# Sample attention of a two-layer decoder step: queries as the 32-column left operand in four column groups, cached keys and values streamed

## The chip, the cores and the metric

The kernel runs on one NeuronCore of a Trainium2 chip. The metric is the device time of one execution in microseconds (us). Three runs of the kernel before gave 3340.89, 3345.87 and 3353.46 us; the median is 3345.87 us.

## The reference, cut to what matters

One inference step goes through two layers for 1024 prompt tokens and for 8 samples of 8 new tokens. The second layer is a dilated sliding-window attention with three groups of heads. The change touches only the samples' part of it:

```python
WINDOWS = (128, 512, 2048)
DILATIONS = (1, 4, 16)
def dilated_group(q, kv, start, dil, n_keys, bias):
    q_pos = start + jnp.arange(Tq)
    idx = q_pos[:, None] - dil * jnp.arange(n_keys)[None, :]
    kvg = kv[:, jnp.maximum(idx, 0)]
    s = jnp.einsum('bqhgd,bqkhd->bqhgk', q, kvg[:, :, :, 0]) * HEAD_DIM ** -0.5
    s = jnp.where(valid[None, :, None, None, :], s + bias, -jnp.inf)
    m = jnp.max(s, axis=-1, keepdims=True)
    p = jnp.exp(s - m)
    l = jnp.sum(p, axis=-1, keepdims=True)
    o = jnp.einsum('bqhgk,bqkhd->bqhgd', (p / l), kvg[:, :, :, 1])
```

A sample's query at token t reads, in group 1 (window 512, step 4), only the cached rows of one residue class modulo 4, and in group 2 (window 2048, step 16) only one of the 8 classes that its 8 tokens need. Group 0 has one class.

## The kernel before, in words

All three groups of the samples are computed in `cross` (L1533), beside the prompt's attention. `cross` walks twelve stages: the groups in the order 2, 1, 0, and in each the four heads of keys c. In a stage `attend` (L1126) computes the prompt's attention for one head and yields at many points; at each yield `advance` (L1550) lets side generators go some steps: `proj_cq` (the next stage's query projection, whose matmuls are recorded at L166, L169 and L170), the sample generators of the group just finished, and in the last group `merge` and the output projection. So the samples of group 2 run beside the prompt's group 1 (1.9 steps to one of `attend`), those of group 1 beside the prompt's group 0 (1.35 steps), and those of group 0 at the end. Within this, a scheduler fixes the order of every engine when the program is built; each engine then runs its list in that order. Weight tiles of the projections, prompt scores (L1172 for group 2, L1174 and L1175 for the others), transposes (L1204, L1116, L1415) and prompt values (L1213) are all in TensorE's one list.

`sample` (L1364) is one sample b of one group g. Its queries are the 128 columns of `qb`, in the order pair p (2), token t (8), then 8 heads. It goes through these steps:

- `fetch(0)` loads the cached keys, L1416 transposes them on TensorE into `kts`, so that they stand as d rows by 128 keys for each class r and pair p.
- L1428: for each class r and pair p, the 128x128 keys are the left operand (the weights) and the few query columns of that class are streamed: 8 columns for group 2, 16 for group 1, 64 for group 0. The helper `cols` picks them. The result `pst` is keys by queries.
- L1430 copies `pst` to SBUF on ScalarE, L1433 transposes it, L1434 adds the scores of the 8 new tokens, L1436 and L1437 add the bias, find the maximum and take the exponential.
- L1440 and L1441 transpose the probabilities; L1442 and L1443 copy them into `pT` and `pTn`.
- L1449 and L1453, both recorded at the helper's L154 (`mmc`, which keeps the matmuls of a chain in order): values as left operand, the 8 or 16 columns of `pT` streamed; then the new tokens' values with 16 rows. L1454 copies the result `po` on ScalarE and L1455 stores it.

All of these are float32. Each float32 matmul that is not a transpose stands in the trace as two records, each with its own weight load; a float32r matmul stands as one. The tiles `pst`, `ps`, `pp`, `po` and the key transposes come from four PSUM banks (tag `aux`), which the prompt's scores use too.

Of the kernel before, what the change touches and what calls it, by code (L numbers as in the profile page):

```python
# [10 lines left out]
AF = mybir.ActivationFunctionType  # L11
ALU = mybir.AluOpType

P = 128
# [93 lines left out]
class Kern:  # L108
# [1255 lines left out]
    def sample(self, g, b, qd, kn, sb, tags):  # L1364

        nc = self.nc
        mm = nc.tensor.matmul
        n = CLASSES[g]
        step = WIN[g] // P

        def fetch(kv):
            cw = self.i[f"cache_win{g + 1}"][b, :, kv].rearrange("(m r) c d -> m r (c d)", r=step)
            res = []
            for x in range(0, n, 4):
                w = min(4, n - x)
                t = self.wslot(tags[x // 4])
                nc.sync.dma_start(out=t[:, :w * 256].rearrange("m (r n) -> m r n", r=w), in_=cw[:, x:x + w])
                res.append(t)
            return res

        def cls(ts, r, p):
            return ts[r // 4][:, (r % 4) * 256 + p * P:(r % 4) * 256 + (p + 1) * P]

        def cols(t, r):
            if g == 0:
                return t
            if g == 2:
                return t[:, r * 8:(r + 1) * 8]
            return t.rearrange("k (e r x) -> k r e x", e=2, r=4)[:, r]

        def half(t, p):
            return t[:, p * 64:(p + 1) * 64]

        if g:
            ks = fetch(0)
            yield
        else:
            kv = self.wslot(tags[0])
            nc.sync.dma_start(out=kv[:, :512], in_=self.i["cache_win1"][b].rearrange("m e c d -> m (e c d)"))
            ks, vs = [kv], [kv[:, 256:512]]  # L1400
            yield
        sc = self.wslot("wh") if self.free and tags[0] == "wh" else self.tl("sc", [P, 656])
        st = pT = o = sc[:, 0:128]
        s, pTn, vn = sc[:, 128:272], sc[0:16, 272:400], sc[0:16, 400:656]
        for p in range(2):
            nc.sync.dma_start(out=vn[p * NS:(p + 1) * NS], in_=self.kvn[g][b * NS:(b + 1) * NS, 256:512])
        kts = []
        for x, src in enumerate(ks):
            t = self.wslot(tags[x]) if g else kv[:, 512:768]
            w = min(1024, n * 256)  # L1410
            for x0 in range(0, w, 512):
                xw = min(512, w)
                pk = self.ps("spp")
                for y in range(0, xw, P):
                    nc.tensor.transpose(pk[:, y:y + P], src[:, x0 + y:x0 + y + P], self.ident)  # L1415
                if x0:  # L1416
                    nc.vector.tensor_copy(t[:, x0:x0 + xw], pk[:, :xw])
                else:
                    nc.scalar.activation(t[:, x0:x0 + xw], pk[:, :xw], AF.Copy)
                yield  # L1420
            kts.append(t)
        if g:
            vs = fetch(1)
        qb = qd[:, b * P:(b + 1) * P]
        pst = self.ps("sa")
        for r in range(n):
            for p in range(2):
                mm(cols(half(pst, p), r), lhsT=cls(kts, r, p), rhs=cols(half(qb, p), r), start=True, stop=True)  # L1428
            yield
        nc.scalar.activation(st, pst[:, :P], AF.Copy)  # L1430
        yield
        ps = self.ps("sa")
        nc.tensor.transpose(ps[:, :P], st, self.ident)  # L1433
        mm(ps[:, P:P + 2 * NS], lhsT=qb, rhs=kn.rearrange("d (p t) -> d p t", p=2)[:, :, b * NS:(b + 1) * NS], start=True, stop=True)  # L1434
        nm, l = self.sml[:, g, 0, b:b + 1], self.sml[:, g, 1, b:b + 1]
        nc.vector.tensor_tensor_reduce(s, ps[:, :P + 2 * NS], sb[:, ::-1], -1.0, 1e38, ALU.add, ALU.min, nm)  # L1436
        nc.scalar.activation(s, s, AF.Exp, bias=nm, scale=-1.0, accum_out=l)  # L1437
        yield
        pp = self.ps("spp")
        nc.tensor.transpose(pp[:, :P], s[:, :P], self.ident)  # L1440
        nc.tensor.transpose(pp[0:2 * NS, P:2 * P], s[:, P:], self.ident)  # L1441
        nc.scalar.activation(pT, pp[:, :P], AF.Copy)  # L1442
        nc.vector.tensor_copy(pTn, pp[0:2 * NS, P:2 * P])  # L1443
        yield
        po = self.ps("spo")
        ch = []
        for p in range(2):
            for r in range(n):
                self.mmc(ch, cols(half(po, p), r), lhsT=cls(vs, r, p), rhs=cols(half(pT, p), r), start=not ch, stop=False)  # L1449
                if r % 2:  # L1450
                    yield
        for p in range(2):
            self.mmc(ch, half(po, p), lhsT=vn[:, p * P:(p + 1) * P], rhs=half(pTn, p), start=False, stop=p == 1)  # L1453
        nc.scalar.activation(o, po[:, :P], AF.Copy)  # L1454
        nc.sync.dma_start(out=self.os[g][:, b * P:(b + 1) * P], in_=o)  # L1455
        yield
# [76 lines left out]
    def cross(self, u):  # L1533
# [38 lines left out]
        self.ready, self.halves = [0] * 4, [[] for _ in range(4)]  # L1572
        self.merged, self.part, self.sampling = 0, [[], []], 4
        marks = []
        q = []
        for _ in self.proj_cq(u, *seq[0], q):
            pass
        for x, (c, g) in enumerate(seq):
# [7 lines left out]
            else:  # L1586
                qn = []
# [30 lines left out]
    def run(self):  # L1618
        tc = self.tc
        self.setup()  # L1620
        self.side, self.ticked = [], 0
        with tc.tile_pool(name="p1", bufs=1) as self.pool:
            self.bufs = {"Y": 16, "Y2": 8, "H": 13, "T": 7}
            self.layer0()
            u = [[None] * 3 for _ in range(KD)]
            late = self.out_proj(0, u, 1, 2)
            u1 = [[None] * 3 for _ in range(KD)]
            late = self.ffn(0, u, late, lambda c, ys: self.finish_norm(c, ys, 3, u1, None))
            self.kv_group(u1, 0, [0])
            self.kv_group(u1, 1, [0])  # L1630
            self.kv_group(u1, 0, [1])
            late()
            self.kv_group(u1, 1, [1])
            self.kv_group(u1, 0, [2])
            self.kv_group(u1, 1, [2])
            self.bias_rows()
            self.kv_group(u1, 2, [0, 1, 2])
        with tc.tile_pool(name="p3", bufs=1) as self.pool:
            self.bufs = {"Q": 6, "KT": 2, "K": 1, "V": 2, "bias": 5, "S": 6, "PT": 4, "row": 2, "st": 3, "ex": 2, "rs": 1, "sel": 1, "qn": 1, "sc": 1}
            self.three = False  # L1640
            self.cross(u1)
            self.three, self.free = True, False
        with tc.tile_pool(name="p4", bufs=1) as self.pool:
            self.bufs = {"Y": 16, "Y2": 8, "H": 13, "T": 7}
            late = self.out_proj(1, u, 5, 6)
            late = self.ffn(1, u, late, self.finish_out)
            late()
        assert not self.shifts
# [65 lines left out]
```

## Time and profile before

| what | before |
|---|---|
| median of 3 runs | 3345.87 us |
| the profiled execution's own time | 3352.04 us |
| its span, first to last instruction | 3350.3 us |
| TensorE matmul busy, share of the span | 97% |
| VectorE / ScalarE busy | 49% / 36% |
| mean granted TensorE clock | 0.979 |
| sample matmuls of groups 1 and 2 (L1428, L154) | first at 1810.5 us, last before 2410 us |

TensorE's busy time is a sum of modelled pipelined records that overlap, so the time that a matmul really takes is read from the start of one to the start of the next, in the timeline. In a timeline row the columns are start, length of the merged records, engine, source line, operation, output and inputs, and the shapes: `128*8` ahead of `128x128` would be rows by columns of the weights, the second shape is the streamed operand. A granted clock of 1.00 is 2.4 GHz, 0.50 is 1.2 GHz.

### The profile page before, as it was taken

To read this page: it belongs to the slowest core of one execution; us is meant where nothing else is said; L and a number is where in the kernel's file an instruction comes from. 1 tells how busy PE (TensorE), PEld (TensorE's weight loads), DVE (VectorE), ACT (ScalarE), POOL (GpSimd) and SP (SyncE) were. 2 spreads that over 40 slices of the span, in tenths; PEclk is the share of its full clock that TensorE was granted. 3 is DMA by queue.
4 is the path that set the end of the run, shared out by engine and by line. 5 is a ranking of instruction groups with operands and counts; after the bars stand their busy time and mean duration, and the time that the engine had idled before them with its cause. 6 is when DMAs were issued, how large, how long until landed. Compare 5 with 4: busy or idle time off the path is not lost.

```text
span 3350.3 us, 51862 instructions
## 1 busy us (share of the span) xinstructions
PE 3262.6 (97%) x20130; PEld 3095.3 (92%) x20130; DVE 1643.8 (49%) x4041; ACT 1220.1 (36%) x3016; POOL 137.3 (4%) x138
## 2 busy tenths in 40 slices
PE   8999999999999999999999999999989999999999
PEld 7899999999999999977888998887788999999998
DVE  5666554533333333462446555766685333333335
ACT  4533334431111111232576665655654211111113
POOL 0000000000000000010000000011111000000000
PEclk9999999999999999999999998988999999999999
DMA  5122234422222222234323443433442322221203
GB/s 179 41 75 73 79 113 156 126 98 70 95 70 82 92 73 70 101 126 135 100 64 95 122 127 85 119 109 92 125 125 91 111 70 88 87 75 63 61 26 110
DMA packets 362410, 318.12 MB, mean 95 GB/s; under 512 B 91208, under 2 KB 346268, under 8 KB 360732
## 3 DMA queue, kind: packets, MB, share of 16 engines
q1 hardware_dynamic: 348472, 302.07, 29.3%
q10 hardware_dynamic: 13596, 12.34, 1.2%
q8 instruction: 158, 2.59, 0.3%
q14 instruction: 88, 0.72, 0.1%
q0 software_dynamic: 96, 0.39, 0.0%
HBM read 251.44 MB, written 107.33 MB: 107 GB/s over the span
## 4 chain that ended last, share of the span: by engine, by line
PE 47%; ACT 3%; DVE 3%; issue 2%; DMA 1%; POOL 1%; SPq 0%; DVEq 0%; ACTq 0%; POOLq 0%
PE mm L166 5%; PE mm L170 5%; PE mm L169 5%; PE aux L166 5%; PE aux L170 5%; PE aux L169 5%; PE mx L1213 2%; PE aux L154 2%; PE mx L170 1%; PE mx L169 1%; PE aux L1428 1%; PE mx L166 1%; PE mx L1204 1%; PE aux L1174 1%; PE nrm L1204 1%
## 5 line engine op out<-in xcount | busy, mean ns | idle before, releaser
L166 PE MATMUL aux<-u,wh 128*128 128x384 f32 (+1 forms) x2112 | 695.8, 330 | 2.5 <-ACT u L220 2.5
L169 PE MATMUL aux<-u,wh 128*128 128x384 f32 (+1 forms) x2112 | 696.1, 330 | 0.0
L170 PE MATMUL aux<-u,wl 128*128 128x384 f32 (+1 forms) x2112 | 695.4, 330 | 0.0
L166 PE MATMUL mm<-u,wh 128*128 128x384 f32 (+1 forms) x1152 | 409.0, 356 | 12.0 <-ACT u L220 10.0
L166 PEld LDWEIGHTS aux<-u,wh 128*128 128x128 f32 x2112 | 397.5, 188 | 3.5 <-ACT u L220 3.5
L169 PEld LDWEIGHTS aux<-u,wh 128*128 128x128 f32 x2112 | 397.6, 188 | 0.3 <-DVE u L221 0.3
L170 PEld LDWEIGHTS aux<-u,wl 128*128 128x128 f32 x2112 | 397.3, 188 | 0.0
L169 PE MATMUL mm<-u,wh 128*128 128x384 f32 (+1 forms) x1152 | 392.5, 341 | 3.3 <-DVE u L221 3.2
L170 PE MATMUL mm<-u,wl 128*128 128x384 f32 (+1 forms) x1152 | 392.6, 341 | 0.0
L926 DVE TENSOR_TENSOR aux<-g,aux 128x384 f32<-128x384 f32 x132 | 71.4, 541 | 610.7 <-PE aux L170 422.6
L91 ACT ACTIVATE wh<-ws 128x1024 fp32r<-128x1024 f32 (+1 forms) x177 | 184.3, 1052 | 445.3 <-PE aux L169 277.5
L92 DVE TENSOR_TENSOR wl<-ws,wh 128x1024 fp32r<-128x1024 f32 (+1 forms) x177 | 215.3, 1225 | 200.2 <-ACT wh L91 199.8
L166 PEld LDWEIGHTS mm<-u,wh 128*128 128x128 f32 x1152 | 223.4, 194 | 23.1 <-ACT u L220 11.5
L169 PEld LDWEIGHTS mm<-u,wh 128*128 128x128 f32 x1152 | 223.0, 194 | 8.7 <-DVE u L221 4.7
L166 PE MATMUL mm<-h,wh 128*128 128x384 f32 (+1 forms) x704 | 230.4, 328 | 0.0
L169 PE MATMUL mm<-h,wh 128*128 128x384 f32 (+1 forms) x704 | 230.3, 327 | 0.0
L170 PE MATMUL mm<-h,wl 128*128 128x384 f32 (+1 forms) x704 | 230.2, 327 | 0.0
L170 PEld LDWEIGHTS mm<-u,wl 128*128 128x128 f32 x1152 | 223.0, 194 | 2.6 <-issue 0.2
L925 ACT ACTIVATE g<-aux 128x384 f32<-128x384 f32 x132 | 61.9, 469 | 432.2 <-PE aux L170 432.2
L945 DVE TENSOR_TENSOR y<-y,mm 128x384 f32<-128x384 f32 (+1 forms) x320 | 168.7, 530 | 101.5 <-PE mm L170 101.3
L927 ACT ACTIVATE h<-aux 128x384 fp32r<-128x384 f32 x132 | 62.0, 469 | 385.9 <-DVE aux L926 385.9
L1179 DVE CUSTOM_DVE_ANT_0 S<-aux,bias 128x128 f32<-128x128 f32 (+1 forms) x384 | 121.6, 349 | 106.6 <-PE aux L1175 44.6
(311 smaller groups left out, 6051.2 us busy)
## 6 DMA issues: line engine op xcount, KB each, us to landing
ws<-in_w_gate_up_dram SPq DMA_DIRECT2D x88, 512.0 KB
out_dram<-in_cache_win_dram SPq DMA_DIRECT2D x64, 510.0 KB
x<-in_cache_win_dram SPq DMA_DIRECT2D x48, 512.0 KB
ws<-in_w_down_dram SPq DMA_DIRECT2D x44, 512.0 KB
ws<-in_w_in_a_dram SPq DMA_DIRECT2D x24, 512.0 KB
ws<-in_w_q_b_dram SPq DMA_DIRECT2D x24, 512.0 KB
hT<-y SPq DMA_DIRECT2D x48, 192.0 KB
og<-row SPq DMA_DIRECT2D x64, 128.0 KB
```

The lines of the kernel that those rows point to most:

```text
L91: nc.scalar.activation(v[1][:, :, :w], v[0][:, :, :w], AF.Copy)
L92: nc.vector.tensor_sub(v[2][:, :, :w], v[0][:, :, :w], v[1][:, :, :w].bitcast(F32))
L154: m = self.nc.tensor.matmul(*args, **kw)
L166: m = mm(out, lhsT=w[0], rhs=x[0], start=start, stop=False)
L169: mm(out, lhsT=w[0], rhs=x[1], start=False, stop=False)
L170: mm(out, lhsT=w[1], rhs=x[0], start=False, stop=stop)
L926: nc.vector.tensor_mul(pu[:, :n], t[:, :n], pu[:, :n])
L927: nc.scalar.activation(h[:, :n], pu[:, :n], AF.Copy)
L945: nc.vector.tensor_add(ys[m][c][:, :n], ys[m][c][:, :n], ps[:, :n])
L1179: nc.vector.tensor_tensor_reduce(s[:, :w], pv, bias[hq][:, :w][:, ::-1], -1.0, 1e38, ALU.add, ALU.min, row[:, hq:hq + 1])
L1204: m = nc.tensor.transpose(pp[:, x * P:(x + 1) * P], pr[hq][:, kt * P:(kt + 1) * P], self.ident)
L1213: m = mm(po, lhsT=v[kt].rearrange("p e d -> p (e d)"), rhs=pT[kt][x], start=x == kt == 0, stop=x == 1 and kt == nk - 1)
```

## The change

Only groups 1 and 2 change; group 0 keeps its code. Scores and values are now both computed by `classes`: the left operand is a slice of 32 columns (of the queries, or of the transposed probabilities), which goes into one of four column groups of the array and writes PSUM partitions 32x to 32x+31; the streamed operand is 128 columns of keys or of values. Four such matmuls (x = 0 to 3, one in each column group) fill one 128x128 block i of a PSUM bank, and i runs over four blocks. A block holds the products of all queries with class i, of which only the rows whose token belongs to the class are wanted. `pick` takes them: four VectorE operations in a chain, each multiplying a block by a 0/1 column of `mine` and adding the sum so far. `mine` is made once in `cross`. For the scores the sum is written into PSUM in place of the transpose of L1433. For the values, the new tokens' product `pn` is copied to SBUF, the four blocks are added to it, and one new transpose turns the result back into the layout that is stored.

```diff
--- before.py
+++ after.py
@@ -1381,13 +1381,6 @@
         def cls(ts, r, p):
             return ts[r // 4][:, (r % 4) * 256 + p * P:(r % 4) * 256 + (p + 1) * P]
 
-        def cols(t, r):
-            if g == 0:
-                return t
-            if g == 2:
-                return t[:, r * 8:(r + 1) * 8]
-            return t.rearrange("k (e r x) -> k r e x", e=2, r=4)[:, r]
-
         def half(t, p):
             return t[:, p * 64:(p + 1) * 64]
 
@@ -1423,14 +1416,43 @@
             vs = fetch(1)
         qb = qd[:, b * P:(b + 1) * P]
         pst = self.ps("sa")
-        for r in range(n):
+
+        def classes(out, left, right):
+
+
+            for i in range(4):
+                for x in range(4):
+                    p, r = x // 2, i if g == 1 else x % 2 * 4 + i
+                    xs = slice(x * 32, x * 32 + 32)
+                    mm(out[xs, i * P:(i + 1) * P], lhsT=left[:, xs], rhs=cls(right, r, p), start=True, stop=True)
+                yield
+                if g == 2:
+                    yield
+
+        def pick(out, src, other, own):
+
+            for i in range(4):
+                dst = out if i == 3 else own
+                if other is None:
+                    nc.vector.tensor_scalar(dst, src[:, :P], self.mine[:, 0:1], None, ALU.mult)
+                else:
+                    nc.vector.scalar_tensor_tensor(out=dst, in0=src[:, i * P:(i + 1) * P], scalar=self.mine[:, i:i + 1],
+                                                   in1=other, op0=ALU.mult, op1=ALU.add)
+                other = own
+
+        if g:
+            yield from classes(pst, qb, kts)
+        else:
             for p in range(2):
-                mm(cols(half(pst, p), r), lhsT=cls(kts, r, p), rhs=cols(half(qb, p), r), start=True, stop=True)
+                mm(half(pst, p), lhsT=cls(kts, 0, p), rhs=half(qb, p), start=True, stop=True)
             yield
-        nc.scalar.activation(st, pst[:, :P], AF.Copy)
+            nc.scalar.activation(st, pst[:, :P], AF.Copy)
         yield
         ps = self.ps("sa")
-        nc.tensor.transpose(ps[:, :P], st, self.ident)
+        if g:
+            pick(ps[:, :P], pst, None, s[:, :P])
+        else:
+            nc.tensor.transpose(ps[:, :P], st, self.ident)
         mm(ps[:, P:P + 2 * NS], lhsT=qb, rhs=kn.rearrange("d (p t) -> d p t", p=2)[:, :, b * NS:(b + 1) * NS], start=True, stop=True)
         nm, l = self.sml[:, g, 0, b:b + 1], self.sml[:, g, 1, b:b + 1]
         nc.vector.tensor_tensor_reduce(s, ps[:, :P + 2 * NS], sb[:, ::-1], -1.0, 1e38, ALU.add, ALU.min, nm)
@@ -1443,13 +1465,21 @@
         nc.vector.tensor_copy(pTn, pp[0:2 * NS, P:2 * P])
         yield
         po = self.ps("spo")
+        if g:
+            yield from classes(po, pT, vs)
+            pn = self.ps("sa")
+            for p in range(2):
+                mm(pn[p * 64:(p + 1) * 64, :P], lhsT=half(pTn, p), rhs=vn[:, p * P:(p + 1) * P], start=True, stop=True)
+            w = s[:, :P]
+            nc.vector.tensor_copy(w, pn[:, :P])
+            pick(w, po, w, w)
+            yield
+            po = self.ps("spp")
+            nc.tensor.transpose(po[:, :P], w, self.ident)
         ch = []
-        for p in range(2):
-            for r in range(n):
-                self.mmc(ch, cols(half(po, p), r), lhsT=cls(vs, r, p), rhs=cols(half(pT, p), r), start=not ch, stop=False)
-                if r % 2:
-                    yield
-        for p in range(2):
+        for p in range(0 if g else 2):
+            self.mmc(ch, half(po, p), lhsT=cls(vs, 0, p), rhs=half(pT, p), start=not ch, stop=False)
+        for p in range(0 if g else 2):
             self.mmc(ch, half(po, p), lhsT=vn[:, p * P:(p + 1) * P], rhs=half(pTn, p), start=False, stop=p == 1)
         nc.scalar.activation(o, po[:, :P], AF.Copy)
         nc.sync.dma_start(out=self.os[g][:, b * P:(b + 1) * P], in_=o)
@@ -1572,6 +1602,9 @@
         self.ready, self.halves = [0] * 4, [[] for _ in range(4)]
         self.merged, self.part, self.sampling = 0, [[], []], 4
         marks = []
+        self.mine = self.tl("mine", [P, 4])
+        self.nc.vector.tensor_reduce(out=self.mine, in_=self.ident.rearrange("p (a i x) -> p i a x", i=4, x=8), op=ALU.add,
+                                     axis=mybir.AxisListType.XY)
         q = []
         for _ in self.proj_cq(u, *seq[0], q):
             pass
@@ -1636,7 +1669,7 @@
             self.bias_rows()
             self.kv_group(u1, 2, [0, 1, 2])
         with tc.tile_pool(name="p3", bufs=1) as self.pool:
-            self.bufs = {"Q": 6, "KT": 2, "K": 1, "V": 2, "bias": 5, "S": 6, "PT": 4, "row": 2, "st": 3, "ex": 2, "rs": 1, "sel": 1, "qn": 1, "sc": 1}
+            self.bufs = {"Q": 6, "KT": 2, "K": 1, "V": 2, "bias": 5, "S": 6, "PT": 4, "row": 2, "st": 3, "ex": 2, "rs": 1, "sel": 1, "qn": 1, "sc": 1, "mine": 1}
             self.three = False
             self.cross(u1)
             self.three, self.free = True, False
```

The built program has 192 matmuls at L1428 and 192 at L154 of groups 1 and 2 before, in 110 uninterrupted runs of TensorE's list. Now it has 512 at L1427, in 102 uninterrupted runs: 63 of four, 17 of eight, and 22 of other lengths. Between a sample's last score matmul and the transpose of its probabilities (L1462) the list now holds some 26 to 78 other matmuls, and between the new tokens' matmuls (L1472) and the new transpose (L1478) some 15 to 33.

TensorE, the scores of the second sample of group 2 before (`mm` is a projection, `mx` the prompt's values, `aux_17632` is `pst`, the `x` tiles are keys and queries):

```order
L170 MATMUL mm_17511<-u_13472,wl_16619 128x384
L1428 MATMUL aux_17632<-x_17105,x_17571 128x8 x4
L1213 MATMUL mx_17637<-PT_17589,V_17142 128x512
L1213 MATMUL mx_17637<-PT_17590,V_17142 128x512
L1213 MATMUL mx_17637<-PT_17618,V_17142 128x512
L166 MATMUL mm_17656<-u_13430,wh_16606 128x384
L1213 MATMUL mx_17637<-PT_17619,V_17142 128x512
L169 MATMUL mm_17656<-u_13431,wh_16606 128x384
L170 MATMUL mm_17656<-u_13430,wl_16607 128x384
L1428 MATMUL aux_17632<-x_17105,x_17571 128x8 x4
```

Four matmuls stand in a run. Each loads 128x128 keys as weights and streams the eight query columns of one class through them.

TensorE, the same place now (`aux_17644` is `pst`):

```order
L1427 MATMUL aux_17644<-x_17583,x_17107 32x128
L1427 MATMUL aux_17644<-x_17608,x_17107 32x128
L1427 MATMUL aux_17644<-x_17583,x_17107 32x128
L1427 MATMUL aux_17644<-x_17608,x_17107 32x128
L1213 MATMUL mx_17649<-PT_17595,V_17144 128x512
L1213 MATMUL mx_17649<-PT_17596,V_17144 128x512
L1213 MATMUL mx_17649<-PT_17620,V_17144 128x512
L1213 MATMUL mx_17649<-PT_17621,V_17144 128x512
L166 MATMUL mm_17668<-u_13430,wh_16608 128x384
L169 MATMUL mm_17668<-u_13431,wh_16608 128x384
L170 MATMUL mm_17668<-u_13430,wl_16609 128x384
L1427 MATMUL aux_17644<-x_17583,x_17107 32x128
```

Each run is four matmuls, one to a column group, and each writes 32 partitions by 128 columns. The program still returns to full-array matmuls between two runs.

VectorE, the same sample's scores before, between the prompt's own work (`rs`, `S`, `Q`, `PT` and `row` are the prompt's):

```order
L1179 ISA rs_17153 128x1
L1207 TENSOR_TENSOR PT_17703<-nrm_17697,PT_17702 128x512
L1207 TENSOR_TENSOR PT_17719<-mx_17713,PT_17718 128x512
L1436 ISA sc_17568,sml<-aux_17742,x_17106 128x144
L1436 ISA sml 128x1
L1075 SCALAR_TENSOR_TENSOR Q_17506<-mm_17656,Q_17506 64x4x32 x2
```

VectorE, the same sample now, between the prompt's own work:

```order
L1207 TENSOR_TENSOR PT_17731<-mx_17725,PT_17730 128x512
L1437 TENSOR_SCALAR sc_17580<-aux_17644,mine_14833 128x128
L1439 SCALAR_TENSOR_TENSOR sc_17580<-aux_17644,mine_14833,sc_17580 128x128 x2
L1439 SCALAR_TENSOR_TENSOR aux_17753<-aux_17644,mine_14833,sc_17580 128x128
L1220 TENSOR_TENSOR row_17547<-mx_17740,row_17547 64x256
L1458 ISA sc_17580,sml<-aux_17753,x_17108 128x144
L1458 ISA sml 128x1
```

The four operations of `pick` stand ahead of the bias and maximum (L1458, an ISA row) and behind the prompt's L1207. Before, L1436 (the same ISA row) was the sample's first operation on VectorE after its score matmuls.

## Rows read from the trace of the kernel before

**Rows 1.** The page: span, busy time, and the two clock and TensorE lines.
```profile
span 3350.3 us, 51862 instructions
PE 3262.6 (97%) x20130; PEld 3095.3 (92%) x20130; DVE 1643.8 (49%) x4041; ACT 1220.1 (36%) x3016; POOL 137.3 (4%) x138
...
PEclk9999999999999999999999998988999999999999
```

**Rows 2.** Table by stretch: length, busy time (instructions) by engine, clock, DMA share, GB/s.
```profile
core 0: us, PE busy (x) PEld busy (x) DVE busy (x) ACT busy (x) POOL busy (x), PEclk, DMA share, GB/s
1620.00:1720.00 100.00, 95.84 (x623) 82.02 (x622) 49.48 (x212) 69.71 (x238) 2.83 (x4) 1.00 0.30 74
1810.00:2110.00 300.00, 295.74 (x1959) 275.34 (x1958) 172.76 (x553) 183.96 (x571) 3.41 (x5) 0.93 0.40 112
2110.00:2410.00 300.00, 287.40 (x1736) 251.50 (x1736) 202.65 (x690) 179.21 (x544) 44.62 (x31) 0.91 0.37 102
```

**Rows 3.** Timeline of TensorE's matmuls around a run of sample values, group 2.
```profile
1834.25 0.34 PE L170 MATMUL mm<-u,wl 128*128 128x384 f32 x1
1834.43 0.95 PE L154 MATMUL aux<-sc,x 128*128 128x8 f32 x8
1835.24 0.42 PE L166 MATMUL mm<-u,wh 128*128 128x384 f32 x1
1835.50 0.34 PE L169 MATMUL mm<-u,wh 128*128 128x384 f32 x1
```

**Rows 4.** Timeline of TensorE's weight loads around the same run.
```profile
1834.25 1.04 PEld L154 LDWEIGHTS aux<-sc,x 128*128 128x128 f32 x8
```

**Rows 5.** Timeline of TensorE's matmuls around a run of prompt scores, group 2.
```profile
1640.27 0.34 PE L169 MATMUL mm<-u,wh 128*128 128x384 f32 x1
1640.44 0.33 PE L170 MATMUL mm<-u,wl 128*128 128x384 f32 x1
1640.70 0.71 PE L1172 MATMUL aux<-KT,Q 64*128 64x128 f32 x8
1641.35 0.44 PE L166 MATMUL mm<-u,wh 128*128 128x384 f32 x1
1641.63 0.34 PE L169 MATMUL mm<-u,wh 128*128 128x384 f32 x1
```

**Rows 6.** Timeline of TensorE's weight loads in the same stretch.
```profile
1640.27 0.19 PEld L170 LDWEIGHTS mm<-u,wl 128*128 128x128 f32 x1
1640.70 0.52 PEld L1172 LDWEIGHTS aux<-KT,Q 64*128 64x128 f32 x8 [0.24 <-issue]
```

**Rows 7.** Timeline and group (busy us, mean ns) of float32 matmuls with 16-column weights.
```profile
1552.32 2.09 PE L383 MATMUL aux<-h,h 33*16 33x384 f32 x6
...
L383 PE MATMUL aux<-h,h 33*16 33x384 f32 x12 | 4.2, 482 | 1.1 <-DMA h<-in_c_onehot_dram 1.0
```

**Rows 8.** Groups of weight loads of 128 and of 16 columns: busy us, mean ns.
```profile
L1440 PEld LDWEIGHTS aux<-ident,sc 128*128 128x128 f32 x20 | 2.8, 139 | 1.1 <-ACT sc L1437 0.5
L1441 PEld LDWEIGHTS aux<-ident,sc 128*16 128x16 f32 x20 | 1.8, 90 | 0.2
```

**Rows 9.** Table by stretch around two falls of the clock: all instructions, columns as Rows 2.
```profile
1894.20:1897.60 3.40, 3.40 (x31) 3.32 (x29) 2.08 (x7) 1.85 (x5) 0.00 (x0) 0.99 0.00 0
1897.60:1907.80 10.20, 10.20 (x42) 9.77 (x42) 2.77 (x13) 4.34 (x15) 0.00 (x0) 0.50 0.13 35
2378.80:2382.20 3.40, 1.73 (x16) 1.43 (x14) 2.91 (x21) 3.40 (x13) 0.00 (x0) 1.00 0.23 84
```

**Rows 10.** The same table for L154 alone: matmul busy, weight-load busy, clock.
```profile
1894.20:1897.60 3.40, 2.42 (x21) 2.48 (x20) 0.99 0.00 0
```

**Rows 11.** Groups of VectorE and ScalarE: busy us, mean ns of one, idle before.
```profile
L1179 DVE CUSTOM_DVE_ANT_0 S<-aux,bias 128x128 f32<-128x128 f32 x208 | 52.2, 287 | 48.0 <-PE aux L1175 16.6 <-PE nrm L1204 12.3 <-PE mx L1204 11.4
L1075 DVE SCALAR_TENSOR_TENSOR Q<-mm,Q 64x128 fp32r<-64x128 f32 x32 | 9.2, 288 | 6.0 <-ACT Q L1074 5.3
L1430 ACT ACTIVATE sc<-aux 128x128 f32<-128x128 f32 x20 | 5.5, 275 | 11.5 <-PE aux L1428 8.6 <-issue 1.6 <-DMA sc<-kvn 1.1
```

**Rows 12.** Waits of TensorE's weight loads, 1810 to 2410 us: total us, times, longest.
```profile
PEld aux L154 <- ACT sc L1442: 2.5, 7, 1.1
...
PEld aux L1433 <- ACT sc L1430: 1.3, 2, 0.9
```

## The prediction

> **What bounds the kernel now.** I read the page first: TensorE's matmuls are busy for 97% of the span, VectorE for 49% and ScalarE for 36% [rows 1], so time goes where TensorE's list gets shorter or longer. The change works only between 1810 and 2410 us, so the table by stretch comes next. There TensorE is busy for 295.74 and 287.40 us of each 300, VectorE for 172.76 and 202.65, and the clock, which is 1.00 in the stretch of prompt attention without samples (1620 to 1720), is 0.93 and 0.91 [rows 2]. Two things can therefore be won: TensorE's own time on the sample matmuls, and the clock. A mean of 0.93 between levels of 1.00 and 0.50 is 0.14 of 300 us at the low level, 0.91 is 0.18 of 300: 42 + 54 = 96 us at 1.2 GHz.
>
> The timelines give the price of one matmul. A run of four sample matmuls (eight records) starts at 1834.43 and the next matmul at 1835.24; the projection matmul behind it takes 0.26 until its successor starts, where 0.175 is usual (from 1834.25 to 1834.43, say). The run costs 0.81 + 0.09 = 0.90 us [rows 3]. The cause is in the weight loads: eight loads of 128 columns take 1.04 us, one after another, while only 8 columns are streamed through each [rows 4]. The array is mostly filled and hardly used.
>
> **The sample matmuls.** Removed are 384 matmuls, 96 times four: 96 x 0.90 = 86 us. Added are 512 with 32-column weights and 128 streamed columns, 128 times four, in 102 runs.
>
> No row shows several column groups at work at once. The nearest is L1172, which splits the array by rows into two halves, also float32 with 128 streamed columns, also four matmuls of two records. From the L170 ahead (1640.44) to the L169 behind (1641.63) are 1.19 us; without the run two steps of 0.175 would stand there, so it costs 0.84 us [rows 5]. What is in it: the first load waits 0.26 us after the last full-array matmul began, instead of starting beside it, and the first matmul behind takes 0.28 us until its successor, where 0.175 is usual [rows 5, 6]. The array is emptied at each change of its division. Between the two edges, eight loads start within 0.33 us (0.52 less the last's 0.19) [rows 6]; eight in turn need 1.04 - 0.19 = 0.85 [rows 4]. So the halves load and compute in pairs: four steps of 0.11 us.
>
> For streaming, L383 has 16-column weights, so that nothing but the stream counts: five steps in 2.09 - 0.48 = 1.61 us, 0.32 for 384 columns, 0.107 for 128 [rows 7]. A record of the new form needs 0.11 us in its group, as one of L1172 did. Its load is smaller; records of 16-column loads last 90 ns against 139 [rows 8]. For the first, unhidden load I take off 0.08 us, an estimate from the 0.11 that a step of 128-column loads takes here.
>
> If the four column groups work at once, four matmuls are two steps instead of four: 0.84 - 0.08 - 2 x 0.11 = 0.54 us for a run, and 0.22 for each further four in it. Rounded up run by run there are 138 fours, so 102 x 0.54 + 36 x 0.22 = 63 us. If they work in turn, four matmuls are eight steps: 0.84 - 0.08 + 4 x 0.11 = 1.20 for a run and 0.88 for a further four, 102 x 1.20 + 26 x 0.88 = 145 us. The bounds are a gain of 23 us and a loss of 59. I take the first, because L1172 shows that parts of the array with weights of their own do run side by side.
>
> On this the Trainium skill has a measurement, in "TensorE: Matmul & The Clock Gate", section "Part 3: Packing small matmuls — row/col tiling": three column groups of 32 gave 2.38 times the speed. No run here shows it yet. At the same yield four groups would give 3.2 times, eight steps of 0.11 would shrink to 0.28 instead of 0.22, and the sum would be 71 us, a gain of 15 in place of 23 (an estimate from that page).
>
> **The clock.** The stretch that ends where the clock falls at 1897.6 had matmuls of L154 busy for 2.42 of its 3.40 us, almost all with 8 columns; then 10.2 us run at 0.50 [rows 9, 10]. Not every fall is like that: ahead of the one at 2382.2 TensorE was busy for only 1.73 of 3.40 us [rows 9]. L1172's 128-column matmuls, with the same emptying at their edges, stand in a stretch at 1.00 [rows 2, 5]. So the new matmuls should bring fewer falls. At most 96 / 2 = 48 us come back, at least none; more falls from the emptied array are part of the rivals. I take half, 24 us, because transposes, merges and emptied arrays stay.
>
> **What VectorE gets.** Per sample nine operations on 128x128 (four, a copy, four). The nearest rows take 287 and 288 ns [rows 11], so 16 x 9 x 0.29 = 42 us more on an engine with some 225 us free in these stretches [rows 2]. ScalarE loses 16 copies of 275 ns [rows 11]. The chain of a sample gets longer: for the scores four operations (1.2 us) replace a copy and a transpose (some 0.4), for the values five operations (1.5 us) come in. What covers it is TensorE's other work: 26 or more matmuls stand behind the scores and mostly some 30 behind the new tokens' values, 3 us and more at 0.11 to 0.18 each. Without that cover it costs 16 x (0.8 + 1.5) = 37 us. Now TensorE waits for the copies of sample chains for 2.5 + 1.3 us in all [rows 12]. Two score tiles are also held in the four `aux` banks during the picks, where ScalarE's copy freed one early; the prompt's scores queue for the same banks. I take 5 us for both, between 0 and 37.
>
> **At nothing:** 16 transposes go and 16 come. The new tokens' 32 matmuls keep their 16 rows and empty the array as before. Making `mine` is one operation. DMAs are the same; no queue is passed.
>
> **The sum:** -23 - 24 + 5 = -42 us. The profiled execution took 3352.04 us, 6 above the median of the runs, so the forecast is 3346 - 42 = 3304 us.
>
> **Rivals.**
> - *Column groups work in turn* (slower). One mechanism: if the second group's load waits for the first group's matmul, four matmuls cost 0.88 us and not 0.22, and the change loses 59 us plus 5 for the picks, less up to 24 of the clock: 3386 to 3410, say 3400. It decides from about 0.45 us per four on, where gain and loss on TensorE cancel. Against it speaks that in L1172 two parts ran at once, and that L170's load runs beside L169's matmul although both use all rows [rows 5, 6]; for it, that only row parts are shown. Chance 0.17. The same page of the Trainium skill ("Part 3", "What overlaps and what doesn't") has a rule that would do it: a load overlaps matmuls in flight only if its row group differs, and column groups share their rows. As a rule for loads in general the trace contradicts it, by the load of L170.
> - *The clock does not recover.* The array is emptied twice in each of 102 runs, and that may look as idle as the thin matmuls. Then -23 + 5 = -18 us: 3328, just about the bound of no change. For it: the fall at 2382.2, ahead of which TensorE was half idle [rows 9]. Chance 0.2.
> - *VectorE becomes the wait.* In the second stretch it has 97 us free of 300 and the merges run there [rows 2]. If the cover fails, +37 in place of +5 leaves -10: 3336. Chance 0.1.
>
> **How the numbers follow.** The forecast case, with half the clock or more and side-by-side groups, has 0.5 and spans 3346 - 23 - 48 = 3275 to some 3325. The remaining 0.03 are surprises on either side. A measurement of this kernel tells about 0.5% (17 us) from no change. Faster by more: 0.5, half of the second rival and a little of the third, 0.63. Within: the rest of those two, 0.17. Slower: the first rival and surprises, 0.20. For 8 in 10 the range runs from 3265, a little beyond the whole clock, to 3365, which is the third rival with another 29 us lost to the banks or the clock; the first rival's price lies outside.
>
> **What would show it.** Loads of L1427 in fours, a few ns apart, and runs of four costing about 0.54 us, edges included: the first step is right. Eight starts some 0.11 us apart: the first rival. A granted clock of 0.95 or more from 1810 to the end of the samples: the second step. TensorE waiting for L1439, or the prompt's L1179 starting late with matmuls of L1174 held behind it: the third rival. A time above 3346 us makes the prediction wrong, whatever the cause.

## The result, and the profile after

| what | before | after |
|---|---|---|
| median (runs) | 3343.38 us (4 runs, 3338.78 to 3353.46) | 3298.51 us (4 runs, 3296.75 to 3304.66) |
| ratio of the two, 95% interval | | 0.9867 [0.9852, 0.9881] |
| the profiled execution's own time | 3352.04 us | 3299.16 us |
| its span | 3350.3 us | 3297.4 us |
| mean granted TensorE clock | 0.979 | 0.989 |

The change makes the kernel 1.3% faster, 45 us by the medians; the interval leaves out 1, and also the 0.5% that the prediction took as the bound of no change. The forecast was 3304 us, 5 above the median. The profiled execution of before was 9 us longer than its median, that of after 1 us, so the two traces differ by 53 us and the medians by 45. The kernel before scatters with its clock: of the 24 runs of it that the experiments are compared with, the longest took 3365.0 us at a mean clock of 0.975, the shortest 3336.87 us at 0.983, and 0.008 of 3350 us are 27 of the 28 us between them.

The page of the kernel after, the lines that answer to [rows 1]:

```profile
span 3297.4 us, 52456 instructions
...
PE 3201.5 (97%) x20386; PEld 2997.8 (91%) x20386; DVE 1679.4 (51%) x4186; ACT 1214.7 (37%) x3000; POOL 138.3 (4%) x138
...
PEclk9999999999999999999999999999999999999999
```

TensorE is still busy for 97%, on a list that is shorter in time. The slices with an 8 in the clock are gone.

The table by stretch of the kernel after, for the two stretches of [rows 2], then from 1800 us to where the samples end and their merge begins (its first transpose stands at 2402.0):

```profile
core 0: us, PE busy (x) PEld busy (x) DVE busy (x) ACT busy (x) POOL busy (x), PEclk, DMA share, GB/s
1810.00:2110.00 300.00, 288.56 (x2255) 238.00 (x2253) 222.83 (x731) 203.70 (x629) 6.60 (x7) 0.99 0.41 116
2110.00:2410.00 300.00, 281.60 (x1970) 234.34 (x1969) 233.85 (x762) 179.15 (x521) 51.02 (x36) 0.97 0.45 132
...
1800.00:2402.00 602.00, 571.30 (x4230) 472.45 (x4229) 458.23 (x1507) 387.51 (x1166) 53.80 (x39) 0.98 0.44 125
```

The same stretch of the kernel before ends with the merge at 2454.5:

```profile
1800.00:2454.50 654.50, 632.41 (x3976) 570.01 (x3975) 422.94 (x1363) 393.28 (x1183) 52.80 (x39) 0.93 0.41 115
```

All of the gain lies here: 654.5 - 602.0 = 52.5 of the 53 us between the traces. Such a row can be taken apart in three. TensorE's gaps are the length less its busy time. The clock's cost is (1 - clock) x length, if what stands in the slow time would take half of it at 2.4 GHz. What is left is TensorE's list at full clock.

| stretch from 1800 us to the merge | length | gaps | clock's cost | list at full clock |
|---|---|---|---|---|
| before | 654.5 | 22.1 | 0.07 x 654.5 = 46 | 586 |
| after | 602.0 | 30.7 | 0.02 x 602.0 = 12 | 559 |
| difference | -52.5 | +9 | -34 | -27 |

The clock is given to two digits, so the last two columns are good to 3 us in a row and move against each other. The list got shorter by some 27 us, the clock gave 34, and 9 us more of gaps took some back. The experiments use the same split.

TensorE's timeline of the kernel after, around a run of sample values of group 2 that stands between projection matmuls:

```profile
1827.04 0.34 PE L170 MATMUL mm<-u,wl 128*128 128x384 f32 x1
1827.31 0.43 PE L1427 MATMUL aux<-x,sc 128*32 128x128 f32 x8
1827.66 0.44 PE L166 MATMUL mm<-u,wh 128*128 128x384 f32 x1
1827.94 0.34 PE L169 MATMUL mm<-u,wh 128*128 128x384 f32 x1
```

And its weight loads:

```profile
1827.30 0.16 PEld L1427 LDWEIGHTS aux<-x,sc 128*32 128x32 f32 x8 [0.26 <-issue]
1827.66 0.19 PEld L166 LDWEIGHTS mm<-u,wh 128*128 128x128 f32 x1 [0.20 <-issue]
```

From the L170 ahead to the L169 behind are 0.90 us; less two usual steps of 0.175, the run costs 0.55. Before it cost 0.90 [rows 3]. Its eight loads stand within 0.16 us, where eight loads of 128 columns took 1.04 [rows 4]. The marks 0.26 and 0.20 are the edges: on either side of the run the next load stands back, where a load between full-array matmuls starts beside the matmul ahead [rows 5, 6]. I read this as the array being emptied before the next weights go in. Within the run nothing stands back: the loads start from 1827.30 on, while the run's own matmuls begin at 1827.31.

### The profile page after: what moved, and what is told of

It reads as the page before. It is cut to its first block, busy times and chain, and to the rows that moved or that the text cites. A ratio compares the mean times of both kernels' runs of the same rounds, so it can differ in the third digit from the quotient of the medians.

```text
span 3297.4 us, 52456 instructions
## 1 busy us (share of the span) xinstructions
PE 3201.5 (97%) x20386; PEld 2997.8 (91%) x20386; DVE 1679.4 (51%) x4186; ACT 1214.7 (37%) x3000; POOL 138.3 (4%) x138
## 4 chain that ended last, share of the span: by engine, by line
PE 44%; DVE 4%; ACT 3%; DMA 2%; issue 2%; POOL 1%; SPq 0%; DVEq 0%; ACTq 0%; POOLq 0%
PE aux L166 5%; PE aux L170 5%; PE aux L169 5%; PE mm L166 5%; PE mm L169 5%; PE mm L170 5%; PE mx L1213 2%; PE mx L170 1%; PE mx L166 1%; PE mx L169 1%; DMA K<-kvs 1%; PE aux L1427 1%; PE nrm L1204 1%; PE mx L1204 1%; ACT S L1181 1%
## 5 line engine op out<-in xcount | busy, mean ns | idle before, releaser
L169 PE MATMUL aux<-u,wh 128*128 128x384 f32 (+1 forms) x2112 | 696.4, 330 | 0.0
L170 PE MATMUL aux<-u,wl 128*128 128x384 f32 (+1 forms) x2112 | 695.8, 330 | 0.0
L166 PE MATMUL mm<-u,wh 128*128 128x384 f32 (+1 forms) x1144 | 397.4, 348 | 6.2 <-ACT u L220 4.3
L169 PEld LDWEIGHTS aux<-u,wh 128*128 128x128 f32 x2112 | 398.1, 189 | 0.0
L170 PEld LDWEIGHTS aux<-u,wl 128*128 128x128 f32 x2112 | 397.9, 188 | 0.0
L169 PE MATMUL mm<-u,wh 128*128 128x384 f32 (+1 forms) x1144 | 387.0, 339 | 0.9 <-DVE u L221 0.6
L170 PE MATMUL mm<-u,wl 128*128 128x384 f32 (+1 forms) x1144 | 385.3, 337 | 0.1
L166 PEld LDWEIGHTS mm<-u,wh 128*128 128x128 f32 x1144 | 218.0, 191 | 19.8 <-ACT u L220 5.5
L169 PE MATMUL mm<-h,wh 128*128 128x384 f32 (+1 forms) x704 | 230.9, 328 | 0.0
L170 PE MATMUL mm<-h,wl 128*128 128x384 f32 (+1 forms) x704 | 230.8, 328 | 0.0
L169 PEld LDWEIGHTS mm<-u,wh 128*128 128x128 f32 x1144 | 217.7, 190 | 7.0 <-DVE u L221 1.9
L170 PEld LDWEIGHTS mm<-u,wl 128*128 128x128 f32 x1144 | 217.7, 190 | 4.5 <-issue 1.3
```

The costliest lines, as they stand in the source:

```text
L166: m = mm(out, lhsT=w[0], rhs=x[0], start=start, stop=False)
L169: mm(out, lhsT=w[0], rhs=x[1], start=False, stop=False)
L170: mm(out, lhsT=w[1], rhs=x[0], start=False, stop=stop)
```

## The experiments

E1 to E4 are compared with one set of runs of the kernel before (3346.24 us, 11 runs), E5 and E6 with a second (3346.53 us, 13 runs).

### E1: the old weights with 128 streamed columns

The kernel before, with its keys and values as weights, but all 128 columns streamed through each.

```diff
-                mm(cols(half(pst, p), r), lhsT=cls(kts, r, p), rhs=cols(half(qb, p), r), start=True, stop=True)
+                if g:
+                    mm(pst[:, :P], lhsT=cls(kts, r, p), rhs=qb, start=True, stop=True)
...
-                self.mmc(ch, cols(half(po, p), r), lhsT=cls(vs, r, p), rhs=cols(half(pT, p), r), start=not ch, stop=False)
+                if g:
+                    self.mmc(ch, po[:, :P], lhsT=cls(vs, r, p), rhs=pT, start=not ch, stop=False)
...
```

> The kernel before, with one thing changed: in groups 1 and 2 each sample matmul streams all 128 query (or probability) columns through its 128x128 weights instead of 8 or 16, so the output is not the reference's (a class's product takes in all tokens). A record is still bound by its weight load (0.11 us, and 128 columns stream in 0.107), so TensorE's own time stays. If the thin streams make the clock fall, the granted clock from 1810 to 2410 us rises from 0.92 to 0.97 or more and the time falls by 20 to 40 us, to 3305 to 3325. If the falls come from the weight loads or from what stands around them, the clock stays at 0.91 to 0.93 and the time at 3335 to 3350.

Measured: 3316.91 us (4 runs, 3314.99 to 3317.2), ratio 0.9906 [0.9891, 0.9921], 29 us faster by the medians. E1's stretch to the merge:

```profile
1800.00:2420.90 620.90, 596.62 (x3969) 541.51 (x3968) 422.69 (x1361) 391.28 (x1180) 54.02 (x39) 0.98 0.43 121
```

TensorE's timeline of E1 around a run of values that stands between projection matmuls, as the one of [rows 3] does:

```profile
2020.76 0.34 PE L170 MATMUL mm<-u,wl 128*128 128x384 f32 x1
2020.93 1.05 PE L154 MATMUL aux<-sc,x 128*128 128x128 f32 x8
2021.74 0.42 PE L166 MATMUL mm<-u,wh 128*128 128x384 f32 x1
2022.01 0.34 PE L169 MATMUL mm<-u,wh 128*128 128x384 f32 x1
```

From the L170 ahead to the L169 behind are 1.25 us; less two usual steps of 0.175, the run costs 0.90, as before: the loads set its pace, and the streamed columns fit beside them. By the split the list is 620.9 - 24.3 - 12 = 584 us, 2 from before's 586, and the gaps are 24.3, 2 more. What fell is the clock's cost, from 46 to 12. So this run shows the clock's part by itself: the matmuls with 8 and 16 streamed columns had brought TensorE to 1.2 GHz at times, and 128 columns through the very same weights gave back 29 us (26 to 36 by the interval). The first reading of the expectation holds, in time and in clock. The change as a whole gains 45; the other 16 are not the clock, and the split of the change has -27 + 9 = -18 us for list and gaps.

### E2: each run of four in one column group

The change, with its two loops exchanged: the four matmuls between two yields now go into the same column group.

```diff
-            for i in range(4):
-                for x in range(4):
+            for x in range(4):
+                for i in range(4):
```

> The changed kernel with its two loops exchanged: the four matmuls of a run now lie in the same column group, so they must go one after another; the result is the same. If the gain rests on four column groups working at once, a run of four takes eight steps of 0.11 us instead of two, 128 x 0.66 = 85 us more: 3365 to 3390, slower than before. If it rests on the smaller weight loads alone, the time stays within 10 us of 3298.

Measured: 3359.94 us (8 runs, 3354.58 to 3364.14), ratio 1.0035 [1.0022, 1.0049]; 61 us over the change. E2's stretch to the merge:

```profile
1800.00:2466.00 666.00, 640.66 (x4234) 544.17 (x4234) 460.48 (x1507) 389.19 (x1168) 54.58 (x39) 0.97 0.39 113
```

TensorE's timeline of E2: two runs of four matmuls (eight records) and one of eight:

```profile
1823.65 1.06 PE L1427 MATMUL aux<-x,sc 128*32 128x128 f32 x8
1824.64 0.44 PE L169 MATMUL mm<-u,wh 128*128 128x384 f32 x1
1824.92 0.34 PE L170 MATMUL mm<-u,wl 128*128 128x384 f32 x1
1825.19 1.06 PE L1427 MATMUL aux<-x,sc 128*32 128x128 f32 x8
...
2132.43 1.53 PE L1427 MATMUL aux<-x,sc 128*32 128x128 f32 x16
```

And the loads of the run at 1825.19:

```profile
1825.19 0.79 PEld L1427 LDWEIGHTS aux<-x,sc 128*32 128x32 f32 x8 [0.25 <-issue]
```

With the same instructions in another order a run of four goes from 0.43 to 1.06 us and its loads from 0.16 to 0.79: this is what matmuls in turn look like, and the change does not. The list is 666.0 - 25.3 - 20 = 621 us, 61 more than after; the clock stays high (0.97).

The expected size was missed: 85 us more was the expectation, 61 came. A run of four costs what was assumed: 0.99 to the next matmul, and 0.10 at either edge (0.27 and 0.28 where 0.175 is usual), 1.19 in all. But 0.88 was assumed for each further four. In E2's longer runs two fours of different column groups stand together, and the row of 16 records takes 1.53 us where 1.06 + 0.88 = 1.94 would be: parts of the two overlap. With 1.53 - 1.06 = 0.47 for a further four, the 100 runs of E2 cost 100 x 1.19 + 28 x 0.47 = 132 us, against some 64 of the change, a difference of 68. The remaining 7 are within what two clocks of two digits allow.

### E3: all sixteen matmuls ahead of the yields

```diff
                     mm(out[xs, i * P:(i + 1) * P], lhsT=left[:, xs], rhs=cls(right, r, p), start=True, stop=True)
+            for i in range(4):
                 yield
                 if g == 2:
                     yield
```

The built program has 48 runs instead of 102, so 54 pairs of edges go.

> The changed kernel with all sixteen matmuls of a class block recorded ahead of the yields instead of four to a yield; the built program then has 48 runs of them instead of 102. If a run's edges (array emptied twice) cost 0.32 us as the prompt's score runs say, 54 x 0.32 = 17 us less: about 3281. If the edges are hidden or the sixteen hold back the prompt's work as much, 3293 to 3310.

Measured: 3301.5 us (4 runs, 3297.09 to 3305.2), ratio 0.9861 [0.9844, 0.9877]: the same as the change. E3's stretch to the merge:

```profile
1800.00:2404.50 604.50, 564.26 (x4245) 481.84 (x4245) 459.23 (x1509) 390.10 (x1170) 54.17 (x39) 0.97 0.44 125
```

TensorE's timeline of E3, a run of all sixteen matmuls:

```profile
1826.40 1.08 PE L1427 MATMUL aux<-x,sc 128*32 128x128 f32 x32
```

The edges did go: the list is 604.5 - 40.2 - 18 = 546 us, 13 less than after. But the gaps are 40.2 us instead of 30.7, and the clock reads 0.97, a cost of 18 us instead of 12, a difference within the rounding. TensorE waits more, and in several places. Two of them, from 1810 to 2410 us, in the kernel after and then in E3 (total us, times, longest): the transposes of the prompt's keys (L1116) wait for the DMA that brings the keys, and the prompt's scores (L1174) for ScalarE's copy of the transposed keys.

```profile
PE nrm L1116 <- DMA K<-kvs: 5.1, 6, 1.5
...
PE aux L1174 <- ACT KT L1122: 1.6, 4, 0.7
```

```profile
PE nrm L1116 <- DMA K<-kvs: 7.6, 5, 2.8
PE aux L1174 <- ACT KT L1122: 2.9, 5, 0.7
```

The time lies in the expectation's second range, 3293 to 3310. Its first reading had taken each edge saved for time saved; the list did lose it, and the waits, with perhaps some of the clock, took it back. The row of 32 records also gives the price of a further four: (1.08 - 0.43) / 3 = 0.22 us, as forecast.

### E4: one pick instead of four

The change with one of the four VectorE operations of each pick.

```diff
-            for i in range(4):
+            for i in (3,):
                 dst = out if i == 3 else own
```

> The changed kernel with one operation of pick instead of four, scores and values: three of the four classes are left out. 16 x 6 operations of 0.35 us, 34 us of VectorE, go. If the picks are mostly covered, the time falls by 0 to 8 us, to 3290 to 3299. If VectorE has become the wait, by 20 us or more, to 3278 or less.

Measured: 3299.82 us (4 runs, 3297.69 to 3301.8), ratio 0.9856 [0.9841, 0.9871]: the same as the change. E4's stretch to the merge:

```profile
1800.00:2401.40 601.40, 576.83 (x4248) 470.98 (x4247) 434.57 (x1413) 390.34 (x1170) 54.03 (x39) 0.99 0.44 126
```

The second reading of the expectation, 3278 us or less, did not come; the first is met within 1 us. VectorE is busy for 24 us less than after, where 34 were expected, and TensorE's gaps are 24.6 instead of 30.7. The end does not move: by the split the clock costs 6 us, 6 less than after, and the list is 601.4 - 24.6 - 6 = 571 us, 12 more. The scheduler has cut the matmuls into 120 runs, 18 more than in the change; 18 further pairs of edges are some 6 of the 12, and for the rest no row here gives a cause. So E4 does not hold the list still, and the picks' own cost is read from the gaps: 6 us at most. Most of these 6 is one wait, that of L1116 for the prompt's keys, 5.1 us in the kernel after and 0.6 in E4:

```profile
PE nrm L1116 <- DMA K<-kvs: 0.6, 1, 0.6
```

That the picks cause this wait is not shown.

### E5 and E6: the scores alone, the values alone

E5 is the change with the values computed as before, E6 with the scores as before. The diff shows E5's switch; the loop over the values of the kernel before follows for all groups, and in E6 the same is done at the scores.

```diff
         po = self.ps("spo")
-        if g:
+        if False:
             yield from classes(po, pT, vs)
...
```

> The changed kernel with the values of groups 1 and 2 computed as before (values as weights, 8 or 16 columns streamed); only the scores are in column groups. If the gain is the sum of two halves, each with its own TensorE time (8 us) and its own share of the falls of the clock, this gives about half, 15 to 28 us less than before: 3318 to 3330, with a granted clock of 0.94 to 0.96 from 1810 to 2410 us. If the thin values alone still make the clock fall as often, the clock stays near 0.92 and the time at 3333 to 3340.

> The changed kernel with the scores of groups 1 and 2 computed as before (keys as weights, thin stream, copy and transpose); only the values are in column groups. Two halves that add up: 3318 to 3330, and with the run of scores only the two gains sum to 40 to 50 us. If the clock needs both gone, the two gains sum to clearly less than 40.

Measured: E5 3334.96 us (10 runs, 3329.82 to 3342.4), ratio 0.9959 [0.994, 0.9977]; E6 3319.92 us (4 runs, 3317.26 to 3331.65), ratio 0.9923 [0.9892, 0.9954]. E5's stretch to the merge, then E6's:

```profile
1800.00:2435.50 635.50, 608.85 (x4066) 524.83 (x4065) 440.16 (x1420) 385.91 (x1161) 52.96 (x39) 0.94 0.41 117
```

```profile
1800.00:2422.20 622.20, 595.22 (x4122) 514.00 (x4121) 443.85 (x1443) 391.91 (x1184) 53.05 (x39) 0.97 0.42 121
```

The scores alone gain 0.41% (14 us, 8 to 20 by the interval), the values alone 0.77% (26 us, 15 to 36); together 40, and the intervals are too wide to tell that from the change's 45. The split of the traces says where the halves differ:

| stretch from 1800 us to the merge | length | gaps | clock's cost | list at full clock |
|---|---|---|---|---|
| E5, scores alone | 635.5 | 26.7 | 0.06 x 635.5 = 38 | 571 |
| E6, values alone | 622.2 | 27.0 | 0.03 x 622.2 = 19 | 576 |

Against before, the list is 15 and 10 us shorter (27 in the change), and the clock costs 8 and 27 us less (34 in the change). So the halves add, as expected, but they are not alike. E5's expectation was missed: its 3334.96 us lies in the range of the other reading (3333 to 3340), while its clock of 0.94 is that of the first. What failed is the equal share of the clock: the scores have some 8 of the 34 us. E6's 3319.92 us is in its range. The thin runs of values (L154) brought most of the slow time, as the stretch ahead of the fall at 1897.6 suggested [rows 9, 10]. Why they more than the scores' runs, which have the same shape, was not tried.

## Why the prediction was right

- **The streams, forecast -23 us.** Right. The step on which all rested was that column groups work side by side, taken over from the row halves of L1172 [rows 5, 6]. A run of four cost 0.55 us (0.54 forecast), a further four 0.22 (0.22 forecast). The list became 27 us shorter, where 23 was forecast, within the rounding of the clock.
- **The yield of a further four.** The Trainium skill's figure in "TensorE: Matmul & The Clock Gate", section "Part 3: Packing small matmuls — row/col tiling", would have made a further four 0.28 us, by an estimate from it. E3's row gives 0.22: here four column groups gave the full factor of four between the edges. The measurement decides.
- **The clock, forecast -24 us of at most 48.** The mechanism was right and the size a little low. E1 shows 29 us from the clock alone [26 to 36 by its interval], and the two traces 34, of which some 8 belong to the trace of before alone (see the sum below). I took half because transposes, merges and emptied arrays stay; no row gave the half, so that it came near is in part luck. The emptied arrays do stay, with a clock of 0.99 and 0.97 in the stretches of [rows 2], so they cost the clock little. The test set for this step, 0.95 or more, holds.
- **Picks and banks, forecast +5 us.** About right in size; how much of it the picks made is not shown. The price of an operation was low: VectorE's pick takes 350 ns, not the 288 of the nearest row [rows 11], so the 16 samples ask for some 16 x 9 x 0.35 = 50 us instead of 42. VectorE's busy time rose by only 35 us, from 422.94 to 458.23. The line of the picks in the kernel after (durations are least, median and most, in ns) and who waited for it (us, times):

```profile
L1439 DVE SCALAR_TENSOR_TENSOR sc<-aux,mine,sc x96: 332/350/353, 1816.6 to 2272.0; 128x128 f32<-128x128 f32 x96
...
  PEld aux L1478: 0.5, 2
  PEld aux L1456: 0.4, 2
```

  TensorE waits for the picks themselves for 0.9 us in all; the cover that the prediction counted, the matmuls behind the scores and the new tokens' values, holds. The longer chain shows a little further on: the weight loads of the transposes of the probabilities wait for the exponential for 3.1 us, where 0.5 were before. The kernel before and then after (total us, times, longest):

```profile
PEld aux L1440 <- ACT sc L1437: 0.5, 2, 0.4
```

```profile
PEld aux L1462 <- ACT sc L1459: 3.1, 7, 1.0
```

  TensorE's gaps grew by 9 us. The largest part with a name is a wait of the prompt that the prediction did not count: that of L1116 for its keys, 5.1 us in the kernel after (see E3) where the kernel before has 1.7:

```profile
PE nrm L1116 <- DMA K<-kvs: 1.7, 2, 1.5
```

- **The sum.** Forecast -23 - 24 + 5 = -42 us; the split of the traces gives -27 - 34 + 9 = -52, and the medians -45. The difference of 7 to 8 is what the profiled execution of before lies further above its median than that of after. The scatter of the runs of before (see the result) speaks for the clock: then the medians are -27 - 26 + 9 = -44 us, and the clock's part is close to the 29 of E1.
- **Column groups in turn (chance 0.17).** Did not happen, and E2 shows what it would have been: 61 us slower than the change, 14 over before. I had said 3400, 40 more than E2. In E2's stretch the list is 35 us longer than before (621 against 586) and not 59: as longer runs overlap, the new matmuls cost 132 us and not 145, and for the other 11 no row gives a cause. The clock gave 26 where I let this rival have some 10. The 0.45 us per four at which gain and loss were to cancel was also wrong by the prediction's own prices: 0.22 + 23 / 138 = 0.39. The rule of the Trainium skill in the same "Part 3", "What overlaps and what doesn't", that a load overlaps matmuls in flight only where its row group differs, would have brought this rival about. The trace contradicts it for column groups too: the eight loads of L1427 use all rows, and they stand within 0.16 us beside matmuls that use all rows too.
- **The clock does not recover (0.2).** Refuted by 0.98 over the whole stretch.
- **VectorE becomes the wait (0.1).** Did not happen: TensorE waits for the picks for 0.9 us, and E4, with three quarters of the pick operations gone, has the same time and at most 6 us less of gaps.

## What to carry to other kernels

Where the trace shows weight loads that take longer than what is streamed through them, two things may be lost, and here they could be won apart: the loads' time, by making the small operand the weights and putting column groups side by side, and the clock, by streaming more columns, even useless ones, through the same loads. The order matters: with four neighbours in one group instead of four, the same instructions lost 61 us, more than the swap gains. And a shorter list need not be a shorter time: E3 took 13 us of edges out and found most of them again as waits for other engines and for DMA.

## What the hardware showed that I had not expected

- Useless columns can be worth more than none. In E1, 128 columns instead of 8 or 16 cost next to no TensorE time (0.90 us for a run in both, the list within 2 us) and returned 29 us through the clock, two thirds of what the whole change gains.
- The fall of the clock came with a full list: TensorE's matmuls were busy for 632 of 654.5 us before, at a mean clock of 0.93, and for 571 of 602 after, at 0.98. A list without gaps did not keep the clock up here, and one with more gaps did not bring it down.
- The edges of a divided array cost some 0.33 us for a run of four (0.55 less 0.22), and E3 paid them once for sixteen, yet 102 such runs leave the clock at 0.98.
